# Decode attention in one layer step: each half of the value columns times its own two heads' weights only, and scores, turned weights and values in single portions

## The chip, the cores and the metric

The kernel runs on one core of one Trainium2 chip. A core has engines that run side by side, each through its own queue of instructions in order: TensorE (PE: matmuls; its weight loads are listed on their own as PEld), VectorE (DVE), ScalarE (ACT), GpSimd (POOL) and SyncE (SP, which here only issues DMAs). Matmuls write to accumulator banks, from which ScalarE and VectorE fetch the results. The metric is device time in microseconds for one execution of the whole program. Before the change it is 994.15 us, the median of three runs (994.03 to 994.83).

## The reference

The program is one layer of a hybrid decoder, applied to a prompt of 512 tokens and to 8 sequences of 8 new tokens each. Input projections feed a gated short convolution and a sliding-window attention; both branches are merged, and a feed-forward network with a short convolution follows. The change touches the attention of the 8 new-token sequences alone, which the reference computes so (16 query heads in 4 groups, one key/value head per group, head width 64, a cache of 128 past rows):

```python
kk = jnp.concatenate([k_buf, k], axis=1)          # 128 cached rows, then the 8 new ones
vv = jnp.concatenate([v_buf, v], axis=1)
s = jnp.einsum('...qhgd,...khd->...hgqk', q, k) * (HEAD_DIM ** -0.5)
s = s - slopes * dist ;  s = where(valid, s, NEG_INF)
m = max(max(s, axis=-1), sink)
p = exp(s - m) ;  p = p / (sum(p) + exp(sink - m))
o = jnp.einsum('...hgqk,...khd->...qhgd', p, v)   # a head's weights meet that head's values only
```

All inputs and outputs are f32.

## The kernel before, in words

**Where the decode attention stands.** The convolution branch is a loop over 8 column blocks (`for m in range(NK)` behind `fill(beside_conv(), 0.19)`). Each block makes three products of the activations `hh`/`hl` (high and low part of h, 128 rows by 576 columns, the columns in two groups of 256 and 320) with weights `whi`/`wlo` into an accumulator `mm`. One step of such a product (`kstep`) is six matmuls, and there are eight steps to a product. After each step `tick()` adds a rate to a counter, and each time the counter passes 1 it takes the next portion from a generator. So TensorE's instructions alternate between product steps and portions of other work. TensorE's order in this phase is that of the program text; the orders of ScalarE and VectorE are made by a planner.

**The generator.** `attention()` first gives the prompt's attention, at a rate of 0.19 portions per step. Then it sets the rate to 0.5 and gives the decode attention; behind it `modulation(2048)` follows at 13/76. Every `yield False` ends a portion. The decode attention works on two groups q of four sequences each:

- `decode_scores` (4 value heads hd = 2j + hf, j and hf each 0 or 1) first turns the cached keys: two portions with four transposes each (`aux<-ident,cKV`), copied by ScalarE to `kTc`. Then come two portions, one for each j, of eight matmuls with 64x32 weights, side by side in the array (`aux<-kTc,qS`), and two with 64x128 weights for the new tokens' keys (`aux<-kT,qS`). They write columns j * 256 on of two banks `S[hf]`. VectorE adds distances and mask into `s` behind each. A fifth portion is the softmax on VectorE and ScalarE, with no matmul.
- `decode_values` turns the weights `s`: two portions (kt = 0 for the cached rows, 1 for the new ones) of four transposes each (`aux<-ident,s`), copied by ScalarE to `pt`. An empty portion follows. Then come two portions, one for each half j of the 256 value columns (a half holds the columns of two heads). In each a bank `O` takes one matmul of the new tokens' values with all 512 columns of `pt[1]` (`aux<-pt,V`), and four of a sequence's cached values with the 128 columns of that sequence in `pt[0]` (`aux<-pt,cKV`: 4 heads by 32 rows). ScalarE then copies the two heads that belong to the half from `O` to `ot` and `oX`, and SyncE stores two pieces.

A half's matmuls thus run over the weights of all four heads, and two heads' results of each half are never read. f32 matmuls appear in the trace as two passes, each with its own weight load.

**The order of portions.** Scores of q=0, scores of q=1, values of q=0, values of q=1: 5 + 5 + 5 + 5 portions. `aux()` gives out four accumulator banks in turn, `mmps()` two larger ones for the products; `slot()` gives out 57 buffers for operands, so the order in which they are asked for sets what a later buffer must wait for. The result `ot` is read again when the attention's output projection begins (`part_o`).

Of the kernel before, what the change touches and what calls it, by code (L numbers as in the profile page):

```python
# [16 lines left out]
P = 128  # L17
# [54 lines left out]
def step_kernel(ctx: ExitStack, tc: tile.TileContext, ins: dict, outs: list):  # L72
# [15 lines left out]
    def nm(s):  # L88
        cnt[0] += 1
        return f"{s}{cnt[0]}"  # L90

    def slot(s, dt=F32, shape=None):
        return ap_.tile(shape or [P, NT], dt, tag="a", name=nm(s))
# [4 lines left out]
    def aux():  # L98
        return pa.tile([P, 512], F32, tag="aux", name=nm("aux"))
# [20 lines left out]
    matmul, transpose = pe.matmul, pe.transpose  # L120
# [73 lines left out]
    filler = []  # L194
# [378 lines left out]
    xn, h, ada1_ps = [], [], {}  # L573
# [184 lines left out]
    def vt(i):  # L758
        return V[i // 2][:, i % 2, :]

    def tok_cols(t, i):

        at = i * P if i < 4 else NT - P
        return t[:, at : at + P]
# [125 lines left out]
    def softmax(s, n, sinks, nsinks, w):  # L890

        nmx = sp.tile([P, n], F32, tag="nmx", name=nm("nmx"))
        for x in range(n // 2):
            nc.vector.tensor_reduce(
                out=nmx[:, 2 * x : 2 * x + 2], in_=s[x][:, :, :w], axis=AX.X, op=ALU.max, negate=True
            )
        nc.vector.tensor_tensor(out=nmx, in0=nmx, in1=nsinks, op=ALU.min)  # L897
        den = sp.tile([P, n], F32, tag="den", name=nm("den"))
        for x in range(n):
            nc.scalar.activation(  # L900
                s[x // 2][:, x % 2, :w], s[x // 2][:, x % 2, :w], AF.Exp,
                bias=nmx[:, x : x + 1], accum_out=den[:, x : x + 1],
            )
        es = sp.tile([P, n], F32, tag="es", name=nm("es"))
        nc.vector.tensor_tensor(out=es, in0=sinks, in1=nmx, op=ALU.add)
        nc.scalar.activation(es, es, AF.Exp)
        nc.vector.tensor_tensor(out=den, in0=den, in1=es, op=ALU.add)
        nc.vector.reciprocal(out=den, in_=den)
        for x in range(n):
            nc.vector.tensor_scalar(  # L910
                out=s[x // 2][:, x % 2, :w], in0=s[x // 2][:, x % 2, :w],
                scalar1=den[:, x : x + 1], scalar2=None, op0=ALU.mult,
            )
# [3 lines left out]
    def cache_load(q):  # L917
        caches[q] = []
        for x in (2 * q, 2 * q + 1):
            for src in ("cache_k_win", "cache_v_win"):  # L920
                t = slot("cKV", shape=[P, 2, 256])
                nc.sync.dma_start(
                    t, ins[src][0, 2 * x : 2 * x + 2].rearrange("b w h d -> w b (h d)")
                )
                caches[q].append(t)

    def decode_scores(q, s, cV):
        kTc = []
        for raw, v in (caches[q][:2], caches[q][2:]):
            cV.append(v)  # L930
            a = aux()
            for b in range(2):
                for j in range(2):
                    at = (b * 2 + j) * P
                    transpose(a[:, at : at + P], raw[:, b, j * P : j * P + P], ident)
            t = slot("kTc", shape=[P, 2, 2, P])
            nc.scalar.copy(t.rearrange("p b j w -> p (b j w)"), a)
            kTc.append(t)
            yield False
        s += [slot("s", shape=[P, 2, 256]) for _ in range(2)]  # L940
        S = [aux() for _ in range(2)]
        for j in range(2):
            at = j * 256
            lhs = qS[:, j, q].rearrange("p b x g t -> p (b x g t)")
            for b in range(4):
                for hf in range(2):
                    matmul(
                        S[hf][32 * b : 32 * b + 32, at : at + P],
                        lhs[HALF[hf], 32 * b : 32 * b + 32],
                        kTc[b // 2][HALF[hf], b % 2, j, :],  # L950
                        start=True, stop=True,
                    )
            for hf in range(2):
                matmul(
                    S[hf][:, at + P : at + 2 * P], lhs[HALF[hf]], tok_cols(kT[j][HALF[hf]], 4),
                    start=True, stop=True,
                )
            for hf in range(2):
                hd = 2 * j + hf
                nc.vector.scalar_tensor_tensor(  # L960
                    out=s[j][:, hf, :], in0=nds[:, q, :], scalar=slo[:, hd : hd + 1],
                    in1=S[hf][:, at : at + 256], op0=ALU.mult, op1=ALU.add,
                )
            yield False
        softmax(s, 4, snks, nsnks, 256)
        yield False

    def decode_values(q, s, cV):
        pt = []
        for kt in range(2):  # L970
            a = aux()
            for hd in range(4):
                transpose(
                    a[:, hd * P : hd * P + P], s[hd // 2][:, hd % 2, kt * P : kt * P + P], ident
                )
            t = slot("pt", shape=[P, 512])
            nc.scalar.copy(t, a)
            pt.append(t)
            yield False
        yield False  # L980
        c = slice(512 + 32 * q, 512 + 32 * q + 32)
        for j in range(2):
            O = aux()
            matmul(O, vt(4)[:, j * P : j * P + P], pt[1], start=True, stop=False)
            p4 = pt[0].rearrange("p (h b r) -> p h b r", h=4, b=4)
            o4 = O.rearrange("p (h b r) -> p h b r", h=4, b=4)
            for b in range(4):
                matmul(
                    o4[:, :, b, :], cV[b // 2][:, b % 2, j * P : j * P + P], p4[:, :, b, :],
                    start=False, stop=(b == 3),  # L990
                )
            oX = slot("oX", shape=[P, 2, 32])
            for hf in range(2):
                src = O[HALF[hf]].rearrange("p (h b x g t) -> p h x g b t", h=4, b=4, x=2, g=2)
                src = src[:, 2 * j + hf]
                dst = ot[j][:, 2 * hf : 2 * hf + 2, c]
                nc.scalar.copy(
                    dst[HALF[hf]].rearrange("p g (b t) -> p g b t", b=4), src[:, hf]
                )
                nc.scalar.copy(  # L1000
                    oX[HALF[hf]].rearrange("p g (b t) -> p g b t", b=4), src[:, 1 - hf]
                )
                nc.sync.dma_start(dst[HALF[1 - hf]], oX[HALF[hf]])
            yield False

    def prompt_ready(hd, i):
        while 4 * hd + 3 not in QS or ticks[0] < ready[hd]:
            yield False
# [35 lines left out]
    def prompt_values(hd, i, pts):  # L1044
        nkt = len(pts)
        O = aux()
        for n in range(2 * nkt):
            kt, par = n // 2, n % 2
            done = nc.tensor.matmul(  # L1049
                O[HALF[par], :256],  # L1050
                vt(i - nkt + 1 + kt)[:, hd * 64 : hd * 64 + 64],
# [6 lines left out]
            ot[hd // 2][:, 2 * (hd % 2) : 2 * (hd % 2) + 2, i * P : i * P + P],  # L1058
            O[:, :256].rearrange("p (g c) -> p g c", g=2),
        )  # L1060

    def attention():


        scored = turned = None
        for n in range(18):
            arg = (n // 4, n % 4) if n < 16 else None
            if n in CACHE_AT:
                cache_load(CACHE_AT.index(n))
            if arg:  # L1070
                yield from prompt_ready(*arg)
            if turned:
                prompt_values(*turned)
            turned = (*scored[:2], prompt_turn(*scored)) if scored else None
            scored = (*arg, []) if arg else None
            if arg:
                prompt_scores(*scored)
            yield False
            if arg:
                h4 = slice(4 * arg[0], 4 * arg[0] + 4)  # L1080
                softmax(scored[2], 4, snk[:, h4], nsnk[:, h4], 256 if arg[1] else P)
            yield False
        filler[1] = 0.5
        waiting = None
        for n in range(3):
            s, more = [], []
            if n < 2:
                yield from decode_scores(n, s, more)
            if waiting is not None:
                yield from waiting  # L1090
            waiting = decode_values(n, s, more) if n < 2 else None
# [108 lines left out]
    def beside_conv():  # L1200
        yield from attention()
        filler[1] = 13 / 76
        yield from modulation(2048)
        yield True
# [749 lines left out]
```

## Time and profile before

| | us |
|---|---|
| median of three runs (lowest, highest) | 994.15 (994.03, 994.83) |
| the profiled execution | 995.13 |
| its span, first to last instruction | 993.4 |
| granted TensorE clock, mean | 0.996 |
| TensorE busy | 977.9 (98%) |
| VectorE busy | 688.8 (69%) |
| ScalarE busy | 464.6 (47%) |
| span 277 to 324 us, with the decode attention | 47.0, all of it TensorE busy |

The profiler's view is of one execution, and times inside it are from the first instruction. "Busy" of TensorE includes modelled ends of matmuls, so distances between the starts of instructions say more than their lengths. The chain of waits follows the work that ended last back from the end. A row of the timeline has the start, the length from the first instruction's start to the last one's end, engine, line, operation, output<-inputs (without buffer numbers), shape and count; L111 is the line of a helper that records most operations, so groups are told apart by their tiles. For matmuls the shape is weights (rows*columns), then the moving operand.

### The profile page before, as it was taken

Reading aid. Unit: us, or ns where it says so; the run is one execution under the profiler, and the core shown is the slowest. Engines: PE = TensorE matmul, PEld = TensorE weight load, DVE = VectorE, ACT = ScalarE, POOL = GpSimd, SP = SyncE. Lnnn points to the kernel's source line nnn. Section 1 sums busy time; section 2 is a strip of 40 time slices with the busy share of each in tenths; the row PEclk is TensorE's granted clock in tenths of the full one; section 3 lists DMA queues with packets and bytes.
Section 4 is the critical chain, followed back from the end, with each engine's and each line's share of the span. In section 5 each row is a group of like instructions: output and inputs, shape, how many; then the busy total and the mean of one; then the engine's idle time right before and its main releaser. Section 6 shows DMA issues by size and latency. Waiting matters only on the chain.

```text
span 993.4 us, 18735 instructions
## 1 busy us (share of the span) xinstructions
PE 977.9 (98%) x7492; PEld 939.1 (95%) x7492; DVE 688.8 (69%) x1289; ACT 464.6 (47%) x861; POOL 103.7 (10%) x275
## 2 busy tenths in 40 slices
PE   7999999999999999999999999999999999999997
PEld 5899999999999989999889999999999999999997
DVE  5736776676452348888578778896569994579853
ACT  5454555555334325454334468653225552245453
POOL 2221101020100000000000032111001110001120
PEclk9999999999999999999999999999999999999999
DMA  9984332243422753234962543433232232323302
GB/s 298 320 245 113 85 87 74 86 116 108 145 68 65 238 191 86 85 86 129 342 221 70 146 110 85 108 102 91 85 107 85 86 89 83 107 77 100 101 10 96
DMA packets 174345, 122.33 MB, mean 123 GB/s; under 512 B 6983, under 2 KB 160942, under 8 KB 173970
## 3 DMA queue, kind: packets, MB, share of 16 engines
q1 hardware_dynamic: 170242, 109.36, 36.3%
q0 software_dynamic: 3872, 11.51, 4.6%
q8 instruction: 59, 0.97, 0.4%
q14 instruction: 28, 0.23, 0.1%
q10 hardware_dynamic: 144, 0.26, 0.1%
HBM read 109.17 MB, written 7.35 MB: 117 GB/s over the span
## 4 chain that ended last, share of the span: by engine, by line
PE 88%; DVE 4%; DMA 3%; issue 2%; ACT 1%; SPq 0%; POOL 0%; POOLq 0%; DVEq 0%; ACTq 0%
PE mm L111 63%; PE aux L111 22%; PE aux L1049 2%; PE aux L1149 1%; DMA ad<-in_w_ada 1%; DVE wlo L111 1%; DMA wlo<-raw 1%; DMA raw<-in_w_in 1%; SPq L418 0%; DVE uv L111 0%; DVE raw L111 0%; DVE y L111 0%; DVE cy L111 0%; ACT whi L111 0%; DVE fl L111 0%
## 5 line engine op out<-in xcount | busy, mean ns | idle before, releaser
L111 ACT ACTIVATE whi<-raw 128x1024 fp32r<-128x1024 f32 (+2 forms) x166 | 170.2, 1034 | 150.6 <-PE mm L111 80.6
L111 DVE TENSOR_TENSOR wlo<-raw,whi 128x1024 fp32r<-128x1024 f32 (+2 forms) x160 | 190.4, 1193 | 47.3 <-ACT whi L111 46.8
L111 PE MATMUL mm<-hh,whi 128*128 128x256 f32 (+2 forms) x560 | 124.7, 299 | 0.6 <-ACT hh L111 0.6
L111 PE MATMUL mm<-hh,wlo 128*128 128x256 f32 (+2 forms) x560 | 121.8, 294 | 0.0
L111 PE MATMUL mm<-hl,whi 128*128 128x256 f32 (+2 forms) x560 | 121.1, 295 | 0.0
L111 PEld LDWEIGHTS mm<-hh,whi 128*128 128x128 f32 x560 | 93.1, 188 | 2.9 <-ACT hh L111 1.2
L111 PEld LDWEIGHTS mm<-hh,wlo 128*128 128x128 f32 x560 | 94.2, 188 | 0.0
L111 PEld LDWEIGHTS mm<-hl,whi 128*128 128x128 f32 x560 | 93.6, 188 | 0.4 <-DVE hl L111 0.4
L111 PE MATMUL mm<-th,whi 128*128 128x288 f32 x224 | 66.6, 297 | 0.4 <-DVE uv L111 0.4
L111 PE MATMUL mm<-th,wlo 128*128 128x288 f32 x224 | 66.1, 295 | 0.0
L111 PE MATMUL mm<-tl,whi 128*128 128x288 f32 x224 | 66.0, 295 | 0.0
L111 PE MATMUL mm<-fl,whi 128*128 128x256 f32 (+1 forms) x304 | 65.2, 295 | 0.0
L111 PE MATMUL mm<-fh,whi 128*128 128x256 f32 (+1 forms) x304 | 64.8, 295 | 0.3 <-DVE rt L111 0.3
L111 PE MATMUL mm<-fh,wlo 128*128 128x256 f32 (+1 forms) x304 | 65.0, 295 | 0.0
L111 DVE SCALAR_TENSOR_TENSOR x<-mm,modT,x 128x512 f32<-128x512 f32 (+1 forms) x29 | 19.6, 676 | 57.7 <-PE mm L111 57.7
L111 PEld LDWEIGHTS mm<-fh,whi 128*128 128x128 f32 x304 | 50.8, 188 | 0.5 <-PE mm L111 0.5
L111 PEld LDWEIGHTS mm<-fl,whi 128*128 128x128 f32 x304 | 50.9, 188 | 0.0
L111 PEld LDWEIGHTS mm<-fh,wlo 128*128 128x128 f32 x304 | 50.9, 188 | 0.0
L900 ACT ACTIVATE s<-s,nmx 128x256 f32<-128x256 f32 (+1 forms) x72 | 34.0, 475 | 32.0 <-DVE nmx L897 31.2
L111 PE MATMUL aux<-2h,whi 128*128 128x288 f32 (+2 forms) x160 | 47.3, 296 | 0.0
L111 PE MATMUL aux<-2l,whi 128*128 128x288 f32 (+2 forms) x160 | 47.3, 295 | 0.0
L111 PE MATMUL aux<-2h,wlo 128*128 128x288 f32 (+2 forms) x160 | 47.2, 295 | 0.0
(332 smaller groups left out, 2610.7 us busy)
## 6 DMA issues: line engine op xcount, KB each, us to landing
raw<-in_w_in SPq DMA_DIRECT2D x52, 512.0 KB, 4.2
raw<-in_w_up SPq DMA_DIRECT2D x44, 512.0 KB, 3.9
ada<-in_w_ada SPq DMA_DIRECT2D x64, 256.0 KB, 5.7
ad<-in_w_ada SPq DMA_DIRECT2D x32, 256.0 KB, 6.3
raw<-in_w_down SPq DMA_DIRECT2D x16, 512.0 KB, 3.6
raw<-in_w_conv_out SPq DMA_DIRECT2D x8, 512.0 KB, 3.5
raw<-in_w_attn_out SPq DMA_DIRECT2D x8, 512.0 KB, 4.7
raw<-in_w_mix_out SPq DMA_DIRECT2D x8, 512.0 KB, 5.1
```

The source lines that it names most:

```text
L111: done = getattr(self.engine, name)(*args, **kwargs)
L900: nc.scalar.activation(s[x // 2][:, x % 2, :w], s[x // 2][:, x % 2, :w], AF.Exp, bias=nmx[:, x : x + 1], accum_out=den[:, x : x + 1],)
L1049: done = nc.tensor.matmul(O[HALF[par], :256], vt(i - nkt + 1 + kt)[:, hd * 64 : hd * 64 + 64], pts[kt][:, par * 256 : par * 256 + 256], st ...
L1149: done = nc.tensor.matmul(ps[32 * j : 32 * j + 32, :], cT[:, k, :], cols[k][j], start=(k == 1), stop=(k == NK - 2),)
```

## The change

1. In `decode_values` a half j multiplies only its own two heads' weights: the moving operand falls from 512 to 256 columns for `aux<-pt,V` and from 128 to 64 for `aux<-pt,cKV`. Both halves write to one bank `O`, half j to columns j * 256 on. The number of matmuls stays.
2. The matmuls of both halves stand in one portion, and the copies and stores of both follow in that portion.
3. Both tiles `pt` are turned in one portion, and both score portions become one, with the four VectorE additions behind all of its matmuls.
4. The rate of portions is 0.35 for 0.5.

The yields of a group fall from 5 to 4 in the scores and from 5 to 3 in the values.

```diff
@@ decode_scores
                     start=True, stop=True,
                 )
+        for j in range(2):
             for hf in range(2):
-                hd = 2 * j + hf
+                hd, at = 2 * j + hf, j * 256
                 nc.vector.scalar_tensor_tensor(
                     out=s[j][:, hf, :], in0=nds[:, q, :], scalar=slo[:, hd : hd + 1],
                     in1=S[hf][:, at : at + 256], op0=ALU.mult, op1=ALU.add,
                 )
-            yield False
+        yield False
         softmax(s, 4, snks, nsnks, 256)
         yield False
@@ decode_values
             nc.scalar.copy(t, a)
             pt.append(t)
-            yield False
+        yield False
         yield False
         c = slice(512 + 32 * q, 512 + 32 * q + 32)
+        O = aux()
+        p4 = pt[0].rearrange("p (h b r) -> p h b r", h=4, b=4)
+        o4 = O.rearrange("p (h b r) -> p h b r", h=4, b=4)
         for j in range(2):
-            O = aux()
-            matmul(O, vt(4)[:, j * P : j * P + P], pt[1], start=True, stop=False)
-            p4 = pt[0].rearrange("p (h b r) -> p h b r", h=4, b=4)
-            o4 = O.rearrange("p (h b r) -> p h b r", h=4, b=4)
+            hs = slice(2 * j, 2 * j + 2)
+            own = slice(j * 256, j * 256 + 256)
+            matmul(O[:, own], vt(4)[:, j * P : j * P + P], pt[1][:, own], start=True, stop=False)
             for b in range(4):
                 matmul(
-                    o4[:, :, b, :], cV[b // 2][:, b % 2, j * P : j * P + P], p4[:, :, b, :],
+                    o4[:, hs, b, :], cV[b // 2][:, b % 2, j * P : j * P + P], p4[:, hs, b, :],
                     start=False, stop=(b == 3),
                 )
+        for j in range(2):
             oX = slot("oX", shape=[P, 2, 32])
...
                 nc.sync.dma_start(dst[HALF[1 - hf]], oX[HALF[hf]])
-            yield False
+        yield False
@@ attention
-        filler[1] = 0.5
+        filler[1] = 0.35
         waiting = None
```

## The prediction

> **What bounds the kernel now.** I read the page first, then the chain of waits and TensorE's timeline over the stretch in which the decode attention runs, then weight loads and matmuls one by one there. On the page (engines' busy times, then the chain by engine):
>
> ```profile
> span 993.4 us, 18735 instructions
> PE 977.9 (98%) x7492; PEld 939.1 (95%) x7492; DVE 688.8 (69%) x1289; ACT 464.6 (47%) x861; POOL 103.7 (10%) x275
> PE 88%; DVE 4%; DMA 3%; issue 2%; ACT 1%; SPq 0%; POOL 0%; POOLq 0%; DVEq 0%; ACTq 0%
> ```
>
> TensorE is busy 98% of the span and carries 88% of the chain. For the stretch the busy times over 276.88 to 323.63 us, and three parts of the chain (start, length, what):
>
> ```profile
> 276.88:323.63 46.75, 46.75 (x400) 42.74 (x399) 22.38 (x46) 19.74 (x53) 1.82 (x6) 1.00 0.21 60
> 277.31 0.44 PE aux L111 x4
> 277.75 1.58 PE mm L111 x12
> ...
> 281.37 0.80 PE aux L111 x20
> 282.17 1.78 PE mm L111 x12
> ...
> 304.56 1.75 PE aux L111 x10
> 306.31 1.59 PE mm L111 x12
> 307.90 1.75 PE aux L111 x10
> ```
>
> All 46.75 us are TensorE's, at a granted clock of 1.00, with VectorE at 22.38 and ScalarE at 19.74. Portions of the decode attention (aux) stand between pieces of the convolution's products (mm), and nothing is waited for. So what TensorE is spared here shortens the stretch, and what it must newly wait for lengthens it. After it the chain stays with TensorE, so I take the shift to reach the end.
>
> **The change, part by part.**
>
> *The value products.* One of today's four value portions (start, length, instructions), and the means of its two forms:
>
> ```profile
> 304.40 1.02 PE L111 MATMUL aux<-pt,V 128*128 128x512 f32 x2
> 305.25 1.05 PE L111 MATMUL aux<-pt,cKV 128*128 128x128 f32 x8
> 306.06 0.52 PE L111 MATMUL mm<-hh,whi 128*128 128x256 f32 x2
> L111 PE MATMUL aux<-pt,cKV 128*128 128x128 f32 x32 | 4.2, 275 | 0.0
> L111 PE MATMUL aux<-pt,V 128*128 128x512 f32 x8 | 4.1, 592 | 0.0
> ```
>
> An f32 matmul runs as two passes: one matmul is x2 here, four are x8. A stated length includes a fixed tail, so I use distances between starts. The two V passes start 1.02 - 0.592 = 0.428 us apart; the eight cache passes (1.05 - 0.275) / 7 = 0.111 us apart. Together 2 x 0.428 + 8 x 0.111 = 1.74 us, and the chain gives the portion 1.75: it has no other cost.
>
> The change halves the columns of every pass and keeps their number (32 cache and 8 V passes). For V the 128-column passes (0.111) against the 512-column ones (0.428) show a cost in proportion to columns, so 256 columns take 0.214: 8 x 0.214 = 1.71 us saved. That is the main term.
>
> The cache passes fall from 128 to 64 columns, but each brings its own 128x128 weights. Two sets of rows bound this: passes of 2 columns with such weights (matmul, then load), and the loads around the only two 64-column passes in full f32 (the second of the two loads, then the next product's):
>
> ```profile
> L111 PE MATMUL aux<-ones,acc 128*128 128x2 f32 x10 | 1.3, 242 | 0.0
> 584.90 0.80 PE L111 MATMUL aux<-ones,acc 128*128 128x2 f32 x6
> 584.87 0.74 PEld L111 LDWEIGHTS aux<-ones,acc 128*128 128x128 f32 x6 [0.18 <-issue]
> 588.10 0.30 PEld L111 LDWEIGHTS aux<-ident,r 128*128 128x128 f32 x2
> 588.32 0.19 PEld L111 LDWEIGHTS mm<-2h,whi 128*128 128x128 f32 x1
> ```
>
> With 2 columns the starts are (0.80 - 0.242) / 5 = 0.112 us apart, no less than with 128. In the other rows the loads start at 588.10, 588.21 (0.30 less one load's 0.19) and 588.32: again 0.11 apart. So the weight load sets 0.11 us per pass below 128 columns, and I take a saving of 0 for the cache passes. The ends: 0 (the 2-column row excludes a loss), and half of 0.111 x 32 = 1.8 us if the columns counted.
>
> The Trainium skill, TensorEngine Tiling (Array Packing), section Instruction Overhead, gives a matmul of one column the time of one of about 60; by that 64 columns would cost half of 128, and the sum below would be 3.9 instead of 2.1. The 2-column row says otherwise for these loads.
>
> Joining the two value portions saves nothing, as there was no cost at their edges. O now takes one accumulator bank for two; its eight copies and four stores stay, but those of the first half now follow both halves' matmuls. Their reader is the split of the attention's output, in the chain 150 us later, which hides that:
>
> ```profile
> 473.14 1.43 DVE ol L111 x2
> ```
>
> *The score portions.* Each q has two; they become one. The first one's chain rows stand above (281.37); its instructions:
>
> ```profile
> 281.30 0.45 PE L111 MATMUL aux<-kTc,qS 64*32 64x128 f32 x16
> 281.67 0.49 PE L111 MATMUL aux<-kT,qS 64*128 64x128 f32 x4
> 282.10 0.53 PE L111 MATMUL mm<-hh,whi 128*128 128x256 f32 x2
> ```
>
> The portion is 0.80 us, and the 12 product matmuls behind it take 1.78 instead of the usual 1.59: 0.99 in all. Its work is eight matmuls of 64x32 weights side by side and two of 64x128 side by side, two passes of 128 columns each: 4 x 0.107 = 0.43 us. The other 0.56 lies at three changes of weight shape (128x128 to 64x32, to 64x128, back): 0.19 each. Two portions have six changes, the joined one five, because its second half begins 64x128 to 64x32. Saved: 2 x 0.19 = 0.38 us. The ends are 0 and all three changes of one portion, 2 x 0.56 = 1.1; I take one change, which the order of matmuls gives.
>
> *The turned weights.* Two portions of four transposes become one of eight. A portion of four is 0.44 us in the chain and the products behind it keep 1.58: no edge to save, 0. The eight need two accumulators at once, freed two portions before.
>
> *The pace.* A portion was due every 2 k-steps (rate 0.5), now every 1/0.35 = 2.86. The generators yield 5 + 5 times per q before and 4 + 3 after, so 20 portions at 0.5 and 14 at 0.35 both end after 40 steps. The modulation behind them stays where it was, and so does every later matmul. In the built order only ScalarE and VectorE work inside this stretch trades places. SyncE's queue keeps its order; its four stores per q come together, and the loads behind them are for products long after.
>
> *The waits.* ScalarE's copy of the second turned key cache of q=1 stands behind the four exponentials of q=0, and TensorE's scores of q=1 wait for it. Today:
>
> ```profile
> 284.79 0.87 DVE L960 SCALAR_TENSOR_TENSOR s<-con,aux 128x256 f32<-128x256 f32 x2 [1.00 <-PE aux L111]
> 285.85 0.69 DVE L1234 TENSOR_TENSOR pad<-mm,c 128x512 f32<-128x512 f32 x1 [0.20 <-PE mm L111]
> 286.59 0.68 DVE L894 TENSOR_REDUCE nmx<-s 128x2 f32<-128x512 f32 x1
> 287.18 1.22 DVE L111 TENSOR_TENSOR wlo<-raw,whi 128x1024 fp32r<-128x1024 f32 x1
> 288.39 0.83 DVE L111 SCALAR_TENSOR_TENSOR y<-pad,parT,y 128x592 f32<-128x592 f32 x1
> 289.07 0.51 ACT L900 ACTIVATE s<-s,nmx 128x256 f32<-128x256 f32 x1
> 291.15 0.57 ACT L937 COPY kTc<-aux 128x512 f32<-128x512 f32 x1
> 292.10 0.45 PE L111 MATMUL aux<-kTc,qS 64*32 64x128 f32 x16
> ```
>
> The copy lands at 291.72, 0.38 us ahead of its reader. After the change VectorE has, from the end of q=0's scores: four additions (2 x 0.87), the pad's products (0.9), two reductions (1.36), wlo 1.22, one y 0.83 and 0.2 for nmx, 6.2 us in all, and then ScalarE's exponentials (291.15 - 289.07 = 2.1) and the copy (0.57): 8.9 us. TensorE gets there after 66 product matmuls (30, 18 and 18) at 1.58 / 12 and two portions of 0.44: 9.6 us. So the copy is still ahead, by 0.7 us, and I charge 0. If that cover is gone, each us of lateness costs one. Every other reader (scores of q=0, turned weights, values) gets a longer gap than today.
>
> **Sum.** 1.71 + 0 + 0.38 + 0 = 2.1 us less. The profiled execution took 995.13 us (its span 993.4 and 1.7 around it), 1 us over the median of 994.15; 993.0 for it, and 994.15 - 2.1 = 992.0 against the median. A measurement tells about 0.2% of this kernel, 2.0 us, from no change, so the sum stands hardly beyond that.
>
> **The rivals.**
>
> *The cache passes halve too* (for: the columns do; against: the 2-column row). 2.1 + 1.8 = 3.9 us: 990.3. This is what the Tiling page's overhead rule in the Trainium skill would make of it.
>
> *The gain falls short.* Products run 576 columns in 1.58 / 6 = 0.263 us, 0.457 ns a column; at that rate 512 columns are 0.234 and the other 0.19 of a V pass would be fixed. Then 256 columns save 0.117, the V term is 0.94 and the sum 1.3: 992.8. Against: a 128-column f32 pass would cost 0.25 then, and costs 0.111. The Trainium skill, TensorE: Matmul & The Clock Gate, section Back-to-back issue gap, has N / 2.4 + 2.5 ns, 216 and 109 ns for 512 and 256 columns; by that the V term would be 0.86. The 0.428 us of this trace is twice its figure, and decides. The likelier way to fall short is a late copy (above) by up to 2 us beyond its cover.
>
> *Slower: the key copy becomes the wait.* It decides from the point where that copy is over 0.7 + 2.1 + 2.0 = 4.8 us later than worked out, at the scores of q=1, for instance when four more long VectorE jobs of 1.22 come ahead of nmx. Time then 996.2 and up. For it: a cover of only 0.38 us today, and a queue in which ScalarE cannot pass the exponentials. Against: VectorE is busy 22.38 of 46.75 us.
>
> **How the numbers follow.** My case 0.62 (its own range 991.5 to 992.6 from 0 to two changes of shape saved per q and the scatter of the runs, 994.03 to 994.83; 0.48 of it beyond 0.2%, 0.14 inside); both halve 0.15; short 0.13, all inside 0.2%; slower 0.10. So faster 0.63, same 0.27, slower 0.10. The range 990.2 to 993.8 takes in the second and third case and leaves out the slower one and a little at either end.
>
> **What would show it.** V passes of 128x256 0.214 us apart, cache passes of 128x64 still 0.11 apart, so that a value portion of 20 passes takes 2.6 us for 3.5 before; a score portion of 40 passes some 1.8 with its edges; no time in the chain for ScalarE or VectorE between 277 and 325 us; the same gaps after. Cache passes 0.055 apart would prove the first rival, a gap on TensorE ahead of the second score portion the last, and V passes over 0.25 apart the fixed share. I am wrong altogether if work far behind the stretch, with its buffers given out in another order, waits anew.

## The result and the profile after

The changed kernel takes 993.19 us (median of 22 runs, 991.93 to 993.85); the kernel before took 994.67 us in the 22 runs beside it. The ratio is 0.9984 with a 95% interval of 0.9977 to 0.9990: faster by 0.16%, 1.5 us between the medians, and the interval holds the 2.1 us of the forecast as well as a gain inside 0.2%.

The profiled execution of the changed kernel took 992.44 us. Its page's head and the engines' busy times:

```profile
span 990.7 us, 18730 instructions
PE 974.7 (98%) x7492; PEld 937.9 (95%) x7492; DVE 687.8 (69%) x1289; ACT 464.8 (47%) x861; POOL 104.2 (11%) x275
```

As many matmuls and weight loads as before, and TensorE is busy 3.2 us less. Of these, 1.1 us lie ahead of the decode attention, where both kernels do the same (270.1 and 269.0 us busy, at a granted clock of 0.99 and 1.00): that belongs to the two executions and not to the change. For the rest, take on TensorE's timeline the stretch from the first transpose of a cached key to the first transpose of the convolution's state. The same product matmuls and the same attention lie in it in both kernels. Before, its two ends were:

```profile
277.15 0.60 PE L111 MATMUL aux<-ident,cKV 128*128 128x128 f32 x4
...
322.60 1.03 PE L111 MATMUL aux<-ident,sto 128*18 128x128 f32 x8
```

After, the two ends, and between them q=0's scores and values and q=1's scores:

```profile
276.77 0.60 PE L111 MATMUL aux<-ident,cKV 128*128 128x128 f32 x4
...
282.48 0.45 PE L111 MATMUL aux<-kTc,qS 64*32 64x128 f32 x16
282.86 0.49 PE L111 MATMUL aux<-kT,qS 64*128 64x128 f32 x4
283.29 0.45 PE L111 MATMUL aux<-kTc,qS 64*32 64x128 f32 x16
...
293.88 0.45 PE L111 MATMUL aux<-kTc,qS 64*32 64x128 f32 x16
...
305.95 0.59 PE L111 MATMUL aux<-pt,V 128*128 128x256 f32 x2
306.38 1.00 PE L111 MATMUL aux<-pt,cKV 128*128 128x64 f32 x8
307.21 0.65 PE L111 MATMUL aux<-pt,V 128*128 128x256 f32 x2
...
320.04 1.04 PE L111 MATMUL aux<-ident,sto 128*18 128x128 f32 x8
```

The stretch was 45.45 us and is 43.27 us: 2.18 us less. The busy times over it:

```profile
276.77:320.04 43.27, 43.27 (x389) 41.42 (x388) 20.95 (x44) 18.69 (x53) 1.57 (x6) 1.00 0.22 63
```

TensorE has every microsecond, as before. That alone does not exclude waits: busy time includes modelled ends, and the experiment with the old rate below has 0.4 us of waits in a stretch that is busy from end to end as well. Equal portions say more. The chain of waits (start, length, what) shows the joined ones, of the scores and the values of each q:

```profile
282.55 1.60 PE aux L111 x40
...
293.95 1.60 PE aux L111 x40
...
306.11 2.59 PE aux L111 x20
...
315.96 2.59 PE aux L111 x20
```

A value portion of 20 passes is 2.59 us (3.5 in two pieces before). The work is the narrow kind: V passes 306.38 - 305.95 = 0.43 us for two, and from the first of eight cache passes to the pass behind them 307.21 - 306.38 = 0.83 us, where it was 306.06 - 305.25 = 0.81 before.

### The profile page after: what moved, and what is told of

Read it like the earlier page. It is cut to its first block, busy times and chain, and to the rows that moved or that the text cites. A ratio compares the mean times of both kernels' runs of the same rounds, so it can differ in the third digit from the quotient of the medians.

```text
span 990.7 us, 18730 instructions
## 1 busy us (share of the span) xinstructions
PE 974.7 (98%) x7492; PEld 937.9 (95%) x7492; DVE 687.8 (69%) x1289; ACT 464.8 (47%) x861; POOL 104.2 (11%) x275
## 4 chain that ended last, share of the span: by engine, by line
PE 91%; DVE 3%; DMA 2%; ACT 2%; issue 1%; POOL 0%; SPq 0%; POOLq 0%; DVEq 0%; ACTq 0%
PE mm L111 65%; PE aux L111 23%; PE aux L1054 2%; PE aux L1154 1%; DVE wlo L111 1%; DMA raw<-in_w_in 1%; DMA wlo<-raw 1%; DMA ad<-in_w_ada 1%; DMA cs<-in_c_prompt 0%; ACT whi L111 0%; DVE uv L111 0%; DVE y L111 0%; DVE raw L111 0%; DVE ol L111 0%; DVE cy L111 0%
```

## The experiments

The theory: a pass of a full-size f32 matmul takes the longer of its columns' time and 0.11 us for its weight load, so only the V passes got shorter; one change of weight shape per q is saved in the scores; nothing waits. The rivals: columns count everywhere; wide passes have a fixed share; portions have edges that cost; the gain is lost behind the stretch. The measure that tells them apart is the stretch above, whose ends can be read to 0.01 us. Three variants (32 columns, one head to a half, the old rate) were executed once each, so of them the stretch alone is read and no time end to end.

### The narrow columns alone

```diff
 (kernel before)
+            hs = slice(2 * j, 2 * j + 2)
+            own = slice(j * 256, j * 256 + 256)
-            matmul(O, vt(4)[:, j * P : j * P + P], pt[1], start=True, stop=False)
+            matmul(O[:, own], vt(4)[:, j * P : j * P + P], pt[1][:, own], start=True, stop=False)
...
-                    o4[:, :, b, :], cV[b // 2][:, b % 2, j * P : j * P + P], p4[:, :, b, :],
+                    o4[:, hs, b, :], cV[b // 2][:, b % 2, j * P : j * P + P], p4[:, hs, b, :],
```

> Half of the change: the kernel before, with each half of the value columns times its own two heads' weights only (256 and 64 columns); two banks, 20 portions and rate 0.5 stay. Measure: the stretch on TensorE from the first transpose of a cached key to the first transpose of the convolution's state (45.45 us before, 43.27 after the whole change). Theory: the eight V passes save 0.214 us each and the 32 cache passes nothing, because their weight loads set the pace: 1.7 us less, 43.75 us. Rival (columns count everywhere): 3.5 us less, 41.95. Rival (the gain comes from joining the portions): under 0.5 us less, about 45.0. End to end the theory has 0.9983 of the time before.

The ends of the stretch in its timeline:

```profile
276.26 0.60 PE L111 MATMUL aux<-ident,cKV 128*128 128x128 f32 x4
...
320.00 1.04 PE L111 MATMUL aux<-ident,sto 128*18 128x128 f32 x8
```

43.74 us, 1.71 less than before: the theory to 0.01 us. End to end 0.9982 (0.9973 to 0.9991), where 0.9983 was expected.

### The joined portions alone

```diff
 (changed kernel)
-        O = aux()
+        Os = [aux() for _ in range(2)]
...
+            o4 = Os[j].rearrange("p (h b r) -> p h b r", h=4, b=4)
-            matmul(O[:, own], vt(4)[:, j * P : j * P + P], pt[1][:, own], start=True, stop=False)
+            matmul(Os[j], vt(4)[:, j * P : j * P + P], pt[1], start=True, stop=False)
...
-                    o4[:, hs, b, :], cV[b // 2][:, b % 2, j * P : j * P + P], p4[:, hs, b, :],
+                    o4[:, :, b, :], cV[b // 2][:, b % 2, j * P : j * P + P], p4[:, :, b, :],
...
```

> The other half: single portions and rate 0.35 as after the change, but all four heads' columns (512 and 128) in both halves, in two banks. Theory: one change of weight shape fewer for each q, 0.2 us each, and nothing at the value and transpose portions: 0.4 us less than the 45.45 of before, 45.05. Rival (edges of portions cost nothing): 45.45. Rival (joining brings waits elsewhere that eat part of the end-to-end gain): stretch as in the theory, but the whole 0.5 us or more slower than before. End to end the theory has 0.9996, which is no measurable difference.

Its stretch runs from 278.08 to 323.05 us. From its chain of waits, a score portion with the products behind it, and a value portion:

```profile
283.86 1.60 PE aux L111 x40
285.46 4.15 PE mm L111 x30
...
307.42 3.50 PE aux L111 x20
```

44.97 us, 0.48 less than before. With the 1.71 above this is 2.19, the whole change's 2.18: the two halves add up. Two separate value portions were 1.75 each, the joined one is 3.50: no edge there. The 30 products behind a score portion take 4.15 us where 30 at the usual 1.58 for 12 take 3.95, so 0.2 of delay stands there once instead of twice: 0.4 of the 0.48. The last 0.08 is spread over the other joints and was not taken apart. End to end 0.9997 (0.9988 to 1.0007), no difference, as expected.

### Cache passes of 32 columns

```diff
 (changed kernel)
-                    o4[:, hs, b, :], cV[b // 2][:, b % 2, j * P : j * P + P], p4[:, hs, b, :],
+                    o4[:, 2 * j, b, :], cV[b // 2][:, b % 2, j * P : j * P + P], p4[:, 2 * j, b, :],
```

> The changed kernel with the cache passes at 32 columns for 64: the second of each half's two heads gets no cached values (that part of the computation is left out). The number of passes and weight loads stays. Theory (the weight load of 0.11 us sets the pace below 128 columns): stretch 43.27 us as after, within 0.1. Rival (a pass has a floor near 60 columns and else goes by columns): also 43.3 but then passes 0.055 apart. Rival (columns count): 32 passes shorter by 0.027 us, 42.4.

```profile
277.16 0.60 PE L111 MATMUL aux<-ident,cKV 128*128 128x128 f32 x4
...
306.76 0.97 PE L111 MATMUL aux<-pt,cKV 128*128 128x32 f32 x8
...
320.42 1.04 PE L111 MATMUL aux<-ident,sto 128*18 128x128 f32 x8
```

43.26 us, as with 64 columns. So neither the step from 128 to 64 nor the one from 64 to 32 shortens the row of these passes. The loads show why; in the changed kernel, between the V and cache passes of one portion (weight loads, start and length):

```profile
306.16 1.08 PEld L111 LDWEIGHTS aux<-pt,cKV 128*128 128x128 f32 x8
307.16 0.30 PEld L111 LDWEIGHTS aux<-pt,V 128*128 128x128 f32 x2
```

The first of the eight loads runs beside the second V pass, 0.214 us; the other seven fill the rest of 307.16 - 306.16 = 1.00: 0.11 us each. A rival is left: each pass could have a floor of 0.11 us of its own, whatever its load. The lengths of single cache passes (shortest, median and longest, in ns) speak against it, with 128 columns (the kernel before), 64 (the changed kernel) and 32:

```profile
L111 PE MATMUL aux<-pt,cKV x32: 272/275/276, 305.3 to 321.7; 128*128 128x128 f32 x32
L111 PE MATMUL aux<-pt,cKV x32: 219/275/275, 306.4 to 318.3; 128*128 128x64 f32 x32
L111 PE MATMUL aux<-pt,cKV x32: 192/276/276, 306.8 to 318.6; 128*128 128x32 f32 x32
```

The shortest is the first pass of a group, whose load ran beside the V pass. It loses 53 ns with 64 columns and another 27 with 32, in proportion to columns; the passes behind it, each with a load to wait for, stay at 275. The rows of eight (1.05, 1.00 and 0.97 us long) lose just these 0.05 and 0.03 us, at their first pass, and what follows them starts no sooner for it. So it is the loads that hold the row at 0.11 us a pass. The Trainium skill, TensorEngine Tiling (Array Packing), section Instruction Overhead, puts the floor of a matmul at about 60 columns; here, with a 128x128 f32 weight load to each pass, a row of passes gains nothing from 128 columns down to 32.

### One head to a half

```diff
 (the kernel of the last experiment)
-            own = slice(j * 256, j * 256 + 256)
+            own = slice(j * 256, j * 256 + 128)
...
-                src = src[:, 2 * j + hf]
+                src = src[:, 2 * j]
```

> The changed kernel with one head in each half for two: V passes of 128 columns for 256 and cache passes of 32 for 64; the second head's results are copies of the first's (its products are left out). Number of passes and loads as before. Theory (a pass takes the longer of its columns at 0.836 ns and its weight load of 0.11 us): the eight V passes fall from 0.214 to 0.11 and the cache passes stay, 8 x 0.103 = 0.82 us less, stretch 42.44 us for 43.26. Rival (full-width passes have their own fixed share of 0.19 us): V passes stay near 0.2, about 43.2. Rival (columns alone): V 0.107 and cache passes 0.027, 39.7.

```profile
277.62 0.60 PE L111 MATMUL aux<-ident,cKV 128*128 128x128 f32 x4
...
306.79 0.38 PE L111 MATMUL aux<-pt,V 128*128 128x128 f32 x2
307.01 0.98 PE L111 MATMUL aux<-pt,cKV 128*128 128x32 f32 x8
...
320.06 1.04 PE L111 MATMUL aux<-ident,sto 128*18 128x128 f32 x8
```

42.44 us, to the hundredth. Two V passes take 307.01 - 306.79 = 0.22 us with 128 columns, 0.43 with 256, 0.86 with 512: no fixed share down to the load's 0.11.

### The changed kernel once more

No edit.

> The changed kernel once more beside the others, to see whether the 2.18 us by which its stretch is shorter reach the end. Theory: all of it does, 0.9978 of the time before, and the first measurement's 0.9984 lies within the scatter. Rival: some 0.6 us are lost behind the stretch, and it comes out near 0.9984 again, with the distances between later groups of the two traces longer by that much.

Its span was 992.3 us, and its stretch ran from 278.59 to 321.85: 43.26 us again.

End to end 0.9983 (0.9974 to 0.9992), much like the first time and not 0.9978, which the interval still holds (the medians, 993.00 beside 995.02 us, lie 2.0 us apart). The trace finds no loss behind the stretch: from the state's transposes to the end of the span were 993.4 - 322.60 = 670.8 us before, and are 990.7 - 320.04 = 670.7 and 992.3 - 321.85 = 670.5 in two executions after. Over all ten traces of this case this part lies between 669.8 and 671.1 us, so one trace scatters by about as much as the rival would lose; but the mean of the nine of other kernels is 670.4, no longer than before. Ahead of the stretch, where the two kernels do the same, its start lies at 277.15 before and at 276.77 and 278.59 after. So single executions differ by up to 2 us before the change begins, as much as it gains. Whether some tenths of the 2.18 us are lost on the way in the median stays open.

### The scores with fewer changes of weight shape

If what joining saves is a change of weight shape, more of them can go. First by order alone:

```diff
 (changed kernel, decode_scores)
+        lhs = [qS[:, j, q].rearrange("p b x g t -> p (b x g t)") for j in range(2)]
         for j in range(2):
...
             for b in range(4):
                 for hf in range(2):
                     matmul(S[hf][32 * b : 32 * b + 32, ...], ..., kTc[...], ...)
+        for j in range(2):
+            at = j * 256
             for hf in range(2):
                 matmul(S[hf][:, at + P : at + 2 * P], lhs[j][HALF[hf]], tok_cols(kT[j][HALF[hf]], 4), ...)
```

> The changed kernel with the joined score portion in another order: the 64x32 matmuls of both j first, then the 64x128 ones of both. Weight shape then changes three times in a portion for five. Theory (what joining the scores saves is one change of weight shape, 0.24 us by the 0.48 measured for two): 2 x 2 x 0.24 = 1.0 us less, stretch 42.3 us for 43.26. Rival (the saving is the edge of a portion, not the shape): no change, 43.26. End to end against the kernel before: 0.9968 by the theory, 0.9978 by the rival.

```profile
276.27 0.60 PE L111 MATMUL aux<-ident,cKV 128*128 128x128 f32 x4
...
281.98 0.67 PE L111 MATMUL aux<-kTc,qS 64*32 64x128 f32 x32
282.57 0.71 PE L111 MATMUL aux<-kT,qS 64*128 64x128 f32 x8
...
318.82 1.04 PE L111 MATMUL aux<-ident,sto 128*18 128x128 f32 x8
```

Then with the new tokens' keys in the 64x32 shape too, four matmuls for one:

```diff
 (changed kernel, decode_scores)
+            for own in (0, 1):
                 for b in range(4):
                     for hf in range(2):
+                        keys = kTc[b // 2][:, b % 2, j, :] if own == 0 else tok_cols(kT[j], 4)
                         matmul(
-                            S[hf][32 * b : 32 * b + 32, at : at + P],
+                            S[hf][32 * b : 32 * b + 32, at + own * P : at + own * P + P],
...
-            for hf in range(2):
-                matmul(S[hf][:, at + P : at + 2 * P], lhs[HALF[hf]], tok_cols(kT[j][HALF[hf]], 4), ...)
```

> The changed kernel with the new tokens' keys also taken by eight 64x32 matmuls for each j instead of two 64x128, so that a score portion has one weight shape and two changes. Theory: three changes fewer for each q, 2 x 3 x 0.24 = 1.4 us less, stretch 41.8 us, and 0.9964 of the time before. Rival (every group of eight costs a load that nothing hides, whatever its shape): 43.3 us.

```profile
277.54 0.60 PE L111 MATMUL aux<-ident,cKV 128*128 128x128 f32 x4
...
283.49 0.42 PE L111 MATMUL aux<-kT,qS 64*32 64x128 f32 x16
283.71 0.48 PE L111 MATMUL aux<-kTc,qS 64*32 64x128 f32 x16
...
319.79 1.04 PE L111 MATMUL aux<-ident,sto 128*18 128x128 f32 x8
```

The order gives 42.55 us, 0.71 less than the changed kernel; one shape gives 42.25, 1.01 less. The cost follows the number of changes: 0.71 / 4 = 0.18 us and 1.01 / 6 = 0.17 us for each. The 0.24 that I expected was the joined portions' 0.48 put down to shape alone; the prediction's 0.19 was nearer. With one shape, groups of 16 passes stand 0.22 us apart, which is twice a pass of 128 columns; with two shapes, 283.29 - 282.86 = 0.43 in the changed kernel. The rival, by which every group pays for a load whatever its shape, is out. What a change consists of was not taken apart. In the changed kernel the loads of the first 64x128 group start together with its passes (both rows at 282.86), not beside the pass before as at 306.16:

```profile
282.86 0.30 PEld L111 LDWEIGHTS aux<-kT,qS 64*128 64x128 f32 x4 [0.20 <-issue]
```

So a load that nothing hides can be part of the 0.18 us. The Trainium skill, TensorEngine Tiling (Array Packing), section Key Properties, says that changing the tiling mode drains TensorE; the runs show a cost of some 0.18 us a time, and not how much of it is the drain. End to end, against the kernel before, 0.9970 (0.9958 to 0.9981) and 0.9965 (0.9953 to 0.9977); medians 991.62 and 991.40 us beside 994.52. Both are clearly faster than the kernel before. Beside the changed kernel neither was measured in one series: their stretches are shorter, and the interval of the second (up to 0.9977) ends where that of the changed kernel (0.9977 to 0.9990) begins.

### The old rate

```diff
 (changed kernel)
-        filler[1] = 0.35
+        filler[1] = 0.5
```

> The changed kernel with the old rate of 0.5: the 14 portions end after 28 steps for 40. TensorE then reaches the scores of q=1 only 48 product matmuls and two portions of 0.44 us after those of q=0, 7.2 us, where the second key copy landed 7.8 us after them in the changed kernel. Theory: TensorE waits there by some 0.6 us, stretch 43.9 us; rival (the slower rate was not needed): 43.26 us and no gap ahead of the second score portion.

ScalarE's second key copy of q=1 and the scores that wait for it, first in the changed kernel (the scores' row, 293.88, stands above), then with the old rate, whose stretch runs from 276.48 to 320.21; there also the copies to `pt` of q=0 and the V passes behind them, and the portions in the chain:

```profile
291.84 0.56 ACT L937 COPY kTc<-aux 128x512 f32<-128x512 f32 x1
```

```profile
289.25 0.57 ACT L937 COPY kTc<-aux 128x512 f32<-128x512 f32 x1
297.79 1.04 ACT L979 COPY pt<-aux 128x512 f32<-128x512 f32 x2
...
289.67 0.63 PE L111 MATMUL aux<-kTc,qS 64*32 64x128 f32 x16
290.23 0.49 PE L111 MATMUL aux<-kT,qS 64*128 64x128 f32 x4
...
298.88 0.70 PE L111 MATMUL aux<-pt,V 128*128 128x256 f32 x2
```

```profile
280.69 1.60 PE aux L111 x40
...
289.74 1.78 PE aux L111 x40
...
298.95 2.79 PE aux L111 x20
```

43.73 us, 0.46 more than with 0.35. At the old rate the copy lands at 289.82, inside the matmuls that need it: 289.67 to 290.23 is 0.56 us for a group that takes 0.38 otherwise, and the portion is 1.78 for 1.60. The value portion of q=0 takes 2.79 for the 2.59 of a joined one, 0.20 longer too: there the copies of the turned weights to `pt` end at 298.83, 0.05 us ahead of the first V pass. The last 0.08 of the 0.46 was not located. So the cover of the key copy is real and short, but the wait came to 0.2 us at that spot, not the 0.6 expected. One reason is that the copy came sooner: it landed 7.5 us behind the end of q=0's scores (282.29), where in the changed kernel it was 8.2 us (292.40 against 284.15; the 7.8 of the expectation is too short). The planner had put VectorE's jobs in another order here, with the products for `pad` behind the reductions.

## Why the prediction was right

- *The value products, 1.71 us from the V passes and 0 from the cache passes.* Measured alone: 1.71. Both halves of the step hold: V passes by columns (0.214 us at 256, 0.11 at 128), cache passes by their weight loads (no change of the row at 64 or 32 columns). The first rival, that the cache passes halve, needed 3.5 us here and is out; so is the fixed share of wide passes. (Of passes with 64 columns the kernel before has four and not two, as the prediction says; the other two stand near 16.4 us, at a granted clock of 0.50, and nothing rests on them.)
- *Joining value portions and transposes: 0.* Value portions 1.75 + 1.75 and 3.50, transposes 0.44 + 0.44 and 0.87: right.
- *Joining the scores: 0.38 us, one change of shape per q.* The joined portions gave 0.48, of which 0.4 stands at the scores; a change of shape measures 0.17 to 0.18 in the experiments that take four and six of them away, against 0.19 in the prediction.
- *The waits: 0.* Right, though not because TensorE is busy through the whole stretch, from which the prediction concluded that nothing is waited for: that view shows no wait with the old rate either. What bears it out is that portions of a kind are equally long for both q (1.60 and 1.60, 2.59 and 2.59), and the copy: put at 0.7 us ahead of its reader, it landed at 292.40 for 293.88, 1.5 us ahead. The working added up the lengths of VectorE's jobs to 6.2 us, and in the trace each begins a little before the one ahead of it ends: the first exponential starts at 289.76, 5.6 us behind the scores. The slower rival was at the right spot: at the old rate that cover is gone and TensorE does wait, by 0.2 us, where by the prediction's sum some 4.1 us of waiting would have decided.
- *Sum and time.* 2.1 us forecast, 2.18 in the trace's stretch, 1.5 in the median of the runs with an interval of 1.0 to 2.3. The time of 993.19 lies 1.2 us over the forecast 992.0: 0.5 because the kernel before came out at 994.67 in the longer series for 994.15 in the three runs, and the rest is the difference between 2.1 and 1.5, which the scatter covers. On which side of 0.2% the change lies is not settled, so the likelier part of the prediction's own case, a gain beyond 0.2%, is neither confirmed nor excluded.

## What to carry to other kernels

In a stretch where TensorE never waits, price passes by the distance between starts, and ask of each whether its columns or its weight load sets the pace: halving the columns paid in full for the 512-wide passes and nothing at all for the 128-wide ones. Look at the changes of weight shape too: keeping matmuls of one shape together, or splitting a few into the shape of their neighbours, shortened the stretch by a further 0.71 and 1.01 us, where the whole change had taken 2.18 off it. And when work is joined into larger portions, check the slowest copy that the next portion waits for; here the slower pace was what kept it covered. A view in which the engine is busy throughout does not show that it never waits: compare equal portions.

## What the runs showed of the hardware

In a row of f32 passes with 128x128 weights of their own each takes 0.11 us, the pace of the weight loads, whether it has 128, 64 or 32 columns; with more columns a pass takes 0.214 us at 256 and 0.428 at 512. The first pass of a row, whose weights are there already, is shorter with fewer columns (272, 219 and 192 ns). A change of weight shape (between 128x128, 64x32 and 64x128) costs about 0.18 us. Four times as many matmuls of 64x32 in place of 64x128 cost TensorE nothing by themselves: a group of 16 passes takes 0.22 us (283.49 to 283.71). The start of the same work, before anything was changed, moved between 276.26 and 278.59 us from one profiled execution to the next.
